# Differential attention heads: each map's scores in one three-bank PSUM tile, with one maximum, one exponential and one combination over 1152 columns

## The chip, the core and the metric

The kernel runs on one core of a Trainium2 chip. A core has a matrix engine (PE, with its weight loads, PEld), a vector engine (DVE), a scalar engine (ACT), GpSimd (POOL), and DMA queues, which are issued from SP here. Each engine works its instructions off in program order and waits on semaphores of the others. Matmul results land in PSUM: 8 banks of 128 partitions x 512 fp32. The metric is the time of one execution in microseconds (us), the median of several runs.

## The reference, cut to what matters

Two layers act on 1152 tokens (128 of a prompt, 1024 of a sample) of width 1024. The first (even) layer is a state-space scan with pooling, the second (odd) layer is attention; the change is in the odd layer's eight differential heads. Each head computes two softmax maps over the same keys and takes one from the other:

```python
def diff_attention(q, k, v, lam):
    scale = DIFF_HD ** -0.5

    def block(qb):
        s = jnp.einsum('bhiqd,bhikd->bhiqk', qb, k).astype(jnp.float32) * scale
        p = jax.nn.softmax(s, axis=-1)
        attn = p[:, :, 0] - lam * p[:, :, 1]
        return jnp.einsum('bhqk,bhkv->bhqv', attn.astype(v.dtype), v)
```

The prompt's 128 queries see 128 keys; the sample's 1024 queries see 1152 keys (1024 of its own and 128 cached ones). Eight pairs of window heads with a sink follow, and an output projection with a residual and a norm.

## The kernel before, in words

Matmuls run in fp16, with every operand split into a high and a low part (three matmuls per product, `mm3`; the score matmuls have both parts of K stacked on the partitions and need two). The PE's order is written out by hand (`manual_schedule`); the orders of DVE, ACT, POOL and SP come from the framework's scheduler, which takes what stands in a `high_priority` block first. Once built, every engine's order is fixed.

`odd` (L1414) lays the work of the odd layer out. `Filler` holds the projections of the next head as generators: 12 chunks per head (k, q, v and the gate z, three chunks of 384 tokens each, each chunk one PSUM bank with 24 matmuls of 384 columns or 72 of 128). `F.take(us)` lays about that much projection work between the attention's matmuls. `diff_head` (L1256) goes through nine blocks of 128 queries: block 0 is the prompt's (128 keys), blocks 1 to 8 have 1152 keys. In a block, for both maps m = 0 and 1:

- Three score chunks of 384 columns (L1280, two matmuls each), each into a bank of its own (`pt("S1")`). Five banks take turns: three of the tag S1, `s4` and `m3`.
- A maximum per chunk on DVE (L1282), a small one over the three (L1286, negated), and an exponential per chunk on ACT (L1289) with its sum, written to SBUF as `p`. A bank is free again once its exponential has read it.
- `F.take(left / 16)`: a sixteenth of the projections that are left. After map 0, also the value products of a block that lies two blocks back (`diff_pv`, 27 matmuls of 128 columns into the bank `sm`, read out by ACT at L1325, squared at L1327).

Then the block is finished: the sums are added (L1298), the factor is built (L1300, L1301), `p[0] + factor * p[1]` is made in three chunks on DVE (L1303), rounded to fp16 on ACT (L1306), the rest taken on POOL (L1307), and both are transposed by a DMA to `PT` (L1227) for the value products.

The projections have two banks (`mm`), one of them being filled while the other is read: by ACT for k and q (L1165, then a shuffle and products on DVE and POOL, L1169 to L1175, and at the end the fp16 copy `qhl`, L1181), by ACT and then DVE for v (L1204, L1205) and z (L1216, L1217). When a head's last value product is in, `diff_pv` builds a reciprocal root on DVE (L1331, then `rsqrt`, L375 to L380, and L1333), and `try_finish` scales nine blocks of the head's output on DVE (L1244 x9); this falls into the first blocks of the next head. New weights are split by ACT (L323) and DVE (L324).

After the eighth head come the window heads (`win_block`), with score banks S1 and value banks `sm` and `s4`; the last two value products of the eighth differential head are laid between the first window blocks' matmuls.

Of the kernel before, what the change touches and what calls it, by code (L numbers as in the profile page):

```python
# [14 lines left out]
ALU = mybir.AluOpType  # L15
# [17 lines left out]
# even layer: the projections between the scans, by group; the fill (us of the tensor engine) of a group and the  # L33
# shares of it before its first step, per stored state, in either half of an output step, and per context state; the
# steps of the storing scan after which M is prepared
# [9 lines left out]
# odd layer: the fill of the first block of a head's queries, behind the first head's projections; the first block of a  # L45
# window head against the others; the score banks
HEAD_FIRST, HEAD_KEEP, HEAD_0 = 1.5, 1.0, 9.0
WIN_FIRST, WIN_SHIFT = 1.5, 1.0
SCORE_BANKS = ("S1", "s4", "S1", "m3", "S1")
NE = 5  # L50
# atanh(z) / z = 1 + s (c0 + c1 s + ...), s = z**2 <= 1/9, to 4e-10
# [20 lines left out]
class Filler:  # L72
    """projections whose matmuls are laid between the attention's and the scans'"""
# [11 lines left out]
    def to_front(self):  # L85
        """the jobs added with front=True from here on come next, behind the one under way"""
        self.pos = 1 if self.begun else 0
# [40 lines left out]
class OutProj:  # L128
    """x_new = x + gate * (g @ w_out), 128 columns of the result at a time; with rby the first half of g is
    scaled by it (per token) on its way out of PSUM"""  # L130
# [21 lines left out]
    def part(self, nb, ps, c0, c1, i):  # L152
        """the i-th k-tile of the order"""
# [6 lines left out]
    def begin(self, n, nb=0):  # L160
        """up to the n-th k-tile of block nb, all chunks of tokens"""
# [24 lines left out]
    def run(self, xres, ssq, chunk_done, chunks, before=None):  # L186
        """the rest; chunk_done(x tiles, first, last token) once a chunk is whole"""
# [34 lines left out]
class Builder:  # L222
# [75 lines left out]
    def pt(self, tag, shape=(P, 512)):  # L298
# [3 lines left out]
        p, b = (self.ps, 2 if tag == "mm" else 1) if tag in ("mm", "m3") else (self.ps2, self.psb[tag])  # L302
        return p.tile(list(shape), F32, tag=tag, bufs=b, name=self.nm("ps" + tag))

    # ---------------------------------------------------------------- weights
    def load_w(self, src, nk=KD, n=P, scale=None, rows=None, pool=None):
        """[128, nk, n] fp32 weights -> (hi, lo) fp16 of 64 * w (* a column scale, or one per k-tile)."""
# [19 lines left out]
    def mm3(self, out, ah, al, bh, bl, start, stop):  # L327
        """out (+)= (ah + al).T @ (bh + bl) without the product of the two low parts"""
# [5 lines left out]
    def g_proj(self, src, hs, evac, pre=None):  # L334
        """channel-major projection: evac(psum [128 ch, 384 tok], first, last token); pre: its weights, and the
# [920 lines left out]
    def diff_head(self, h, F):  # L1256
# [8 lines left out]
        for b in range(NCH):  # L1265
# [30 lines left out]
            with self.tc.high_priority():  # L1296
# [8 lines left out]
                for c0, c1 in part:  # L1305
                    nc.scalar.activation(phl[:, c0:c1], p[0][:, c0:c1], AF.Copy)  # L1306
# [337 lines left out]
```

## Time and profile before

| what | value |
|---|---|
| time, median of 3 runs | 2302.61 us (2298.39 to 2303.87) |
| profiled execution, from the first to the last instruction | 2299.9 us, granted PE clock 0.958 on the mean |
| PE busy over the span | 2025.4 us (88%) |
| DVE busy | 1658.4 us (72%) |
| ACT busy | 1275.3 us (55%) |
| POOL busy | 1070.7 us (47%) |
| first score matmul of the differential heads | at 1023.1 us |
| first score matmul of the window heads | at 1709.3 us |

A row of a group reads: line, engine, operation, output tile <- input tiles, shapes, count | busy us, mean ns of one | idle time of the engine just before, and what ended it. A row of a timeline reads: start, length, engine, line, tiles, and in brackets the idle time before it with what ended that. PE's lengths overlap: matmuls are pipelined, and the pitch from start to start is what one costs. A window's row gives each engine's busy time and count, the granted PE clock, the DMA share and GB/s.

### The profile page before, as it was taken

How to read it: one execution, taken by the hardware profiler on the slowest of the kernel's cores; microseconds unless marked ns; L12 is line 12 of the kernel's file. 1: busy time of each engine (PE TensorE's matmuls, PEld its weight loads, DVE VectorE, ACT ScalarE, POOL GpSimd, SP SyncE). 2: the span in 40 equal slices, each digit the busy share in tenths (PEclk: the TensorE clock that was granted, in tenths of full speed). 3: DMA queues.
4: the chain of work that ended last, by engine and by line, in shares of the span. 5: the costliest groups of instructions: out<-in, count | busy, mean ns of one | idle time of the engine just before them, and what ended most of it. 6: DMA issues, size and time to landing. Idle time of an engine off the chain costs nothing. (4 is left out here: it accounts for less than half of the span.)

```text
span 2299.9 us, 51010 instructions
## 1 busy us (share of the span) xinstructions
PE 2025.4 (88%) x20258; PEld 1449.5 (63%) x20258; DVE 1658.4 (72%) x3483; ACT 1275.3 (55%) x3432; POOL 1070.7 (47%) x997
## 2 busy tenths in 40 slices
PE   5997788788999999989898898998978898988997
PEld 2654475654657555657586686676666777676566
DVE  5878989789585544768978978878888767663334
ACT  5575656666464211447666666676667756673321
POOL 1378677876774100154534435445446656552001
PEclk9998899998999999999999999999999999999999
DMA  7221514224657412136445455455466867889412
GB/s 283 63 82 53 152 46 122 78 82 132 224 180 209 172 63 85 63 100 121 98 109 123 90 121 121 89 122 110 96 121 137 162 145 152 168 170 206 147 47 83
DMA packets 434990, 283.17 MB, mean 123 GB/s; under 512 B 374432, under 2 KB 385216, under 8 KB 434752
## 3 DMA queue, kind: packets, MB, share of 16 engines
q1 hardware_dynamic: 433776, 279.34, 49.0%
q8 instruction: 158, 2.59, 0.5%
q10 hardware_dynamic: 976, 0.58, 0.1%
q14 instruction: 80, 0.66, 0.1%
HBM read 133.38 MB, written 29.05 MB: 71 GB/s over the span
## 5 line engine op out<-in xcount | busy, mean ns | idle before, releaser
L330 PE MATMUL psmm<-h,whl 128*128 128x384 f16 (+1 forms) x1104 | 366.4, 333 | 9.7 <-DVE V L1205 3.8
L331 PE MATMUL psmm<-h,whl 128*128 128x384 f16 (+1 forms) x1104 | 365.7, 332 | 2.4 <-DVE h L507 1.7
L332 PE MATMUL psmm<-h,whl 128*128 128x384 f16 (+1 forms) x1104 | 365.1, 332 | 0.0
L330 PE MATMUL psmm<-whl,h 128*128 128x128 f16 x1920 | 346.2, 225 | 0.0
L331 PE MATMUL psmm<-whl,h 128*128 128x128 f16 x1920 | 345.8, 224 | 0.0
L332 PE MATMUL psmm<-whl,h 128*128 128x128 f16 x1920 | 345.5, 224 | 0.0
L331 PEld LDWEIGHTS <-whl 128*128 128x128 f16 x2256 | 224.8, 100 | 155.4 <-issue 30.7
L332 PEld LDWEIGHTS <-whl 128*128 128x128 f16 x2256 | 224.4, 99 | 155.1 <-issue 16.0
L330 PEld LDWEIGHTS <-whl 128*128 128x128 f16 x2256 | 225.5, 100 | 149.4 <-issue 21.5
L1307 POOL TENSOR_TENSOR phl<-p,phl 128x1152 f16<-128x1152 f32 (+1 forms) x72 | 158.4, 2200 | 242.4 <-ACT phl L1306 208.7
L324 DVE SCALAR_TENSOR_TENSOR whl<-w,whl 128x512 f16<-128x512 f32 x248 | 211.3, 875 | 67.8 <-ACT whl L323 67.4
L330 PEld LDWEIGHTS <-h 128*128 128x128 f16 x2520 | 251.2, 100 | 9.5 <-issue 3.8
L331 PEld LDWEIGHTS <-h 128*128 128x128 f16 x2520 | 251.1, 100 | 7.6 <-issue 1.9
L332 PEld LDWEIGHTS <-h 128*128 128x128 f16 x2520 | 250.9, 100 | 0.0
L1289 ACT ACTIVATE p<-psS,sms 128x384 f32<-128x384 f32 (+1 forms) x240 | 136.4, 570 | 100.3 <-DVE sms L1286 100.2
L1387 POOL TENSOR_TENSOR phl<-p,phl 128x1024 f16<-128x1024 f32 (+2 forms) x72 | 134.2, 1864 | 120.4 <-ACT phl L1386 120.1
L323 ACT ACTIVATE whl<-w 128x512 f16<-128x512 f32 x248 | 140.0, 609 | 81.3 <-PE psmm L332 44.7
L1173 POOL TENSOR_TENSOR sw<-sw,sin 128x384 f32<-128x384 f32 (+1 forms) x78 | 84.7, 1087 | 147.7 <-DVE sw L1172 134.9
L1280 PEld LDWEIGHTS <-Q 128*128 128x128 f16 x800 | 73.7, 98 | 126.0 <-issue 91.3
L504 POOL TENSOR_TENSOR h<-mt,h 128x384 f16<-128x384 f32 (+2 forms) x32 | 29.3, 925 | 251.6 <-ACT h L503 251.6
L1280 PE MATMUL psS<-K,Q 128*128 128x384 f16 (+1 forms) x480 | 109.5, 323 | 41.6 <-ACT p L1289 41.4
L1303 DVE SCALAR_TENSOR_TENSOR p<-p,sms,p 128x384 f32<-128x384 f32 (+1 forms) x200 | 136.7, 718 | 2.0
(394 smaller groups left out, 6242.5 us busy)
## 6 DMA issues: line engine op xcount, KB each, us to landing
w<-in_wod SPq DMA_DIRECT2D x52, 512.0 KB, 3.7
w<-in_wev SPq DMA_DIRECT2D x40, 512.0 KB, 4.1
E<-csrow SPq DMA_DIRECT2D x36, 512.0 KB, 4.0
Q<-qhl SPq DMA_DIRECT2D x64, 288.0 KB, 4.5
go_dr<-gl SPq DMA_DIRECT2D x15, 576.0 KB, 3.2
wada<-in_w_ada SPq DMA_DIRECT2D x32, 256.0 KB, 5.8
o<-in_w_ada SPq DMA_DIRECT2D x16, 512.0 KB, 5.9
xT<-in_w_ada SPq DMA_DIRECT2D x16, 512.0 KB, 5.9
```

Source lines behind the costliest of these rows:

```text
L323: nc.scalar.activation(hl[:, 0, a:e], w[:, a:e], AF.Copy if scale is None else AF.Identity, scale=sc)
L324: nc.vector.scalar_tensor_tensor(hl[:, 1, a:e], w[:, a:e], sc, hl[:, 0, a:e], ALU.mult, ALU.subtract)
L330: mm(out, ah, bh, start=start, stop=False)
L331: mm(out, ah, bl, start=False, stop=False)
L332: mm(out, al, bh, start=False, stop=stop)
L504: nc.gpsimd.tensor_tensor(h[:, 1, a:b], o, h[:, 0, a:b], ALU.subtract)
L1173: nc.gpsimd.tensor_tensor(sw[:, o:], sw[:, o:], self.sinT[:, a:b], ALU.mult)
L1280: nc.tensor.matmul(sv, q[:, m, x, qs], k[:, m, o + c0:o + c1], start=x == 0, stop=x == 1)
L1289: nc.scalar.activation(pm[:, c0:c1], ss[j], AF.Exp, bias=nb, accum_out=sm[:, i:i + 1])
L1303: nc.vector.scalar_tensor_tensor(p[0][:, c0:c1], p[1][:, c0:c1], sm[:, 2:3], p[0][:, c0:c1], ALU.mult, ALU.add)
L1307: nc.gpsimd.tensor_tensor(phl[:, w:2 * w], p[0][:, :w], phl[:, :w], ALU.subtract)
L1387: nc.gpsimd.tensor_tensor(phl[:, 2 * w:4 * w], p, phl[:, :2 * w], ALU.subtract)
```

## The change

The score banks of the differential heads become two tiles of three banks each (tag `S`, 6 banks). A map's scores for all 1152 columns go into one tile (matmuls of 512, 512 and 128 columns). One maximum and one exponential run over the whole row. Map 0's exponential goes to SBUF as before; map 1's is written back over its own scores in PSUM and read from there by one combination of 1152 columns, and one fp16 copy follows. The chunk maxima's reduction and the adding of the chunk sums go. The other two banks (`mm`) serve the projections and, in turn with them, the value products. When the eight heads are done, all value products that still wait are issued, the pool of `S` tiles is closed, and the window heads get banks as before. `m3` is a bank of the even layer's pool, and then of the window heads' pool.

```diff
@@ pt
-        p, b = (self.ps, 2 if tag == "mm" else 1) if tag in ("mm", "m3") else (self.ps2, self.psb[tag])
+        p, b = (self.ps, 2) if tag == "mm" else (self.ps2, self.psb[tag])
@@ prologue
-        self.evps.enter_context(self.psum("evps", ss=4, ada=1))
+        self.evps.enter_context(self.psum("evps", ss=4, ada=1, m3=1))
@@ diff_head
+            o = TC if b else 0
-            sm = self.wt([P, 16], F32, tag="sms", bufs=6)
-            part = ((0, P),) if b == 0 else CH3
+            sm = self.wt([P, 8], F32, tag="sms", bufs=6)
             for m in range(2):
-                ss = []
-                mx = self.wt([P, 4], F32, tag="mx", bufs=4)
+                sv = self.pt("S", [P, 1536])[:, :w]
                 nb = sm[:, m:m + 1]
-                for j, (c0, c1) in enumerate(part):
-                    sv = self.pt("S1")[:, :c1 - c0]
-                    o = TC if b else 0
+                for c0 in range(0, w, 512):
+                    c1 = min(c0 + 512, w)
                     for x in range(2):
-                        nc.tensor.matmul(sv, q[:, m, x, qs], k[:, m, o + c0:o + c1], start=x == 0, stop=x == 1)
-                    with self.tc.high_priority():
-                        nc.vector.tensor_reduce(out=mx[:, j:j + 1], in_=sv, axis=AX.X, op=ALU.max)
-                    ss.append(sv)
-                pm = self.wt([P, T], F32, tag="p", bufs=4)
+                        nc.tensor.matmul(sv[:, c0:c1], q[:, m, x, qs], k[:, m, o + c0:o + c1], start=x == 0, stop=x == 1)
+                e = self.wt([P, T], F32, tag="p", bufs=4)[:, :w] if m == 0 else sv
                 with self.tc.high_priority():
-                    nc.vector.tensor_reduce(out=nb, in_=mx[:, 0:len(part)], axis=AX.X, op=ALU.max, negate=True)
-                    for j, (c0, c1) in enumerate(part):
-                        i = 8 + m * 3 + j
-                        nc.scalar.activation(pm[:, c0:c1], ss[j], AF.Exp, bias=nb, accum_out=sm[:, i:i + 1])
-                p.append(pm)
+                    nc.vector.tensor_reduce(out=nb, in_=sv, axis=AX.X, op=ALU.max, negate=True)
+                    nc.scalar.activation(e, sv, AF.Exp, bias=nb, accum_out=sm[:, 4 + m:5 + m])
+                p.append(e)
...
-                n = len(part)
-                nc.vector.tensor_reduce(out=sm[:, 4:6], in_=sm[:, 8:14].rearrange("p (a b) -> p a b", a=2)[:, :, 0:n],
-                                        axis=AX.X, op=ALU.add)
                 nc.vector.reciprocal(sm[:, 6:8], sm[:, 4:6])
                 nc.vector.scalar_tensor_tensor(sm[:, 2:3], sm[:, 4:5], self.nlam, sm[:, 7:8], ALU.mult, ALU.mult)
-                for c0, c1 in part:
-                    nc.vector.scalar_tensor_tensor(p[0][:, c0:c1], p[1][:, c0:c1], sm[:, 2:3], p[0][:, c0:c1],
-                                                   ALU.mult, ALU.add)
-                for c0, c1 in part:
-                    nc.scalar.activation(phl[:, c0:c1], p[0][:, c0:c1], AF.Copy)
-            nc.gpsimd.tensor_tensor(phl[:, w:2 * w], p[0][:, :w], phl[:, :w], ALU.subtract)
+                nc.vector.scalar_tensor_tensor(p[0], p[1], sm[:, 2:3], p[0], ALU.mult, ALU.add)
+                nc.scalar.activation(phl[:, :w], p[0], AF.Copy)
+            nc.gpsimd.tensor_tensor(phl[:, w:2 * w], p[0], phl[:, :w], ALU.subtract)
@@ odd
-                odps.enter_context(self.psum("odps", S1=3, s4=1, sm=1))
-                self.banks = {"mm": ["m3", "S1", "mm", "mm"]}
+                odps.enter_context(self.psum("dfps", S=2))
+                self.banks = {"mm": ["S", "S", "mm", "mm"]}
...
-                self.banks = {"mm": ["mm"], "S1": list(SCORE_BANKS)}
+                self.banks = {"mm": ["mm"], "sm": ["mm"]}
...
                     self.diff_head(h, F)
+                F.until(("wk", 0))
+                F.until(("q", 8))
+                self.pop(0)
+                odps.close()
+                odps.enter_context(self.psum("odps", S1=3, m3=1, s4=1, sm=1))
                 self.banks = {"mm": ["mm", "mm", "m3"], "sm": ["sm", "s4"]}
```

The rest of the diff drops comments and blank docstrings, so the line numbers of the changed kernel lie a little lower: L1281 is its maximum, L1282 its exponential, L1292 its combination, L1293 its fp16 copy, L1312 the read-out of the value product, L1164 that of a k or q chunk, L1203 that of a v chunk, L1243 the scaling of the head's output. On the PE the change moves nothing: matmul by matmul the same products stand in the same places, with other tiles and other score widths. On ACT and DVE the scheduler lays the rows in another order.

The first place is DVE in the fourth block of the fourth head, where the third head's output is scaled. `psS` are scores, `p` the exponentials of map 0, `raw` and `sw` belong to a q chunk, `og` is the head's output. Before:

```order
L1282 TENSOR_REDUCE mx_16466<-psS_1996_16475 128x1
L1244 SCALAR_TENSOR_TENSOR og_14606<-og_14606,orr_16335,zs_15558 128x128
L1286 TENSOR_REDUCE sms_16421<-mx_16466 128x1
L1244 SCALAR_TENSOR_TENSOR og_14606<-og_14606,orr_16335,zs_15558 128x128 x2
...
L1282 TENSOR_REDUCE mx_16524<-psS_2005_16525 128x1
L1282 TENSOR_REDUCE mx_16524<-pss_2006_16529 128x1
L1282 TENSOR_REDUCE mx_16524<-psS_2007_16533 128x1
L1300 RECIPROCAL sms_16421<-sms_16421 128x2
L1244 SCALAR_TENSOR_TENSOR og_14606<-og_14606,orr_16335,zs_15558 128x128
L1286 TENSOR_REDUCE sms_16523<-mx_16524 128x1
...
L1303 SCALAR_TENSOR_TENSOR p_16435<-p_16479,sms_16421,p_16435 128x384 x3
```

And in the changed kernel, at the same place of the PE's order (its `psS_15862` and `psS_15906` are the score rows that before had 16467 to 16475 and 16525 to 16533):

```order
L1243 SCALAR_TENSOR_TENSOR og_14242<-og_14242,orr_15753,zs_15070 128x128 x5
L1281 TENSOR_REDUCE sms_15825<-psS_15862 128x1
L1243 SCALAR_TENSOR_TENSOR og_14242<-og_14242,orr_15753,zs_15070 128x128
L1171 STREAM_SHUFFLE sw_15879<-raw_15877 128x384
L1173 TENSOR_TENSOR q_1775_15707<-raw_15877,cos_11480 128x384
L1243 SCALAR_TENSOR_TENSOR og_14242<-og_14242,orr_15753,zs_15070 128x128
L1290 RECIPROCAL sms_15825<-sms_15825 128x2
L1243 SCALAR_TENSOR_TENSOR og_14242<-og_14242,orr_15753,zs_15070 128x128
L1291 SCALAR_TENSOR_TENSOR sms_15825<-sms_15825,lms_11493 128x1
L1292 SCALAR_TENSOR_TENSOR p_15833<-psS_15862,sms_15825,p_15833 128x1152
L1281 TENSOR_REDUCE sms_15905<-psS_15906 128x1
```

Before, the next block's maxima stand ahead of this block's combination; now the next block's maximum stands behind the combination, and six of the nine products of L1243 (the first of them one row ahead of these) ahead of this block's second maximum.

The second place is ACT there, up to the read-out of a value product (`og`). `psmm_16497` and `psmm_15884` are the same chunk of q, before and now. Before:

```order
L1289 ACTIVATE p_16479,sms_16421<-psS_1996_16475,sms_16421 128x384
L1289 ACTIVATE p_16537,sms_16523<-psS_2005_16525,sms_16523 128x384
L1289 ACTIVATE p_16537,sms_16523<-pss_2006_16529,sms_16523 128x384
L1165 ACTIVATE raw_16554<-psmm_16497 128x384
L323 ACTIVATE whl_17439<-w_2102_17437 128x512 x2
L1289 ACTIVATE p_16537,sms_16523<-psS_2007_16533,sms_16523 128x384
L1306 ACTIVATE phl_16510<-p_16435 128x384 x3
L1181 ACTIVATE qhl_16561<-q_1965_16289 128x1152
L1325 ACTIVATE og_16015<-pssm_16596,sms_16116 128x128
```

Now:

```order
L1282 ACTIVATE psS_15862,sms_15825<-psS_15862,sms_15825 128x1152
L509 ACTIVATE gl_15778<-og_14242 128x1152
L1293 ACTIVATE phl_15897<-p_15833 128x1152
L1282 ACTIVATE p_15913,sms_15905<-psS_15906,sms_15905 128x1152
L1164 ACTIVATE raw_15928<-psmm_15884 128x384
L322 ACTIVATE whl_16709<-w_1865_16707 128x512 x2
L1180 ACTIVATE qhl_15935<-q_1775_15707 128x1152
L1312 ACTIVATE og_15469<-psmm_15970,sms_15564 128x128
```

The chunk's read-out now stands behind the fp16 copy of the block before it and behind a whole row's exponential. The value product `psmm_15970` (before: `pssm_16596`, in a bank of its own) takes the bank that `psmm_15884` had, since the other of the two is being filled by the next chunk.

The third place is ACT where the last two v chunks of a head are read out (`V`). Before:

```order
L1325 ACTIVATE og_16015<-pssm_16785,sms_16242 128x128
L1327 ACTIVATE osq_16814,oss_16016<-og_16015 128x128
L1289 ACTIVATE p_16829,sms_16709<-psS_2037_16817,sms_16709 128x384
L1204 ACTIVATE V_16569<-psmm_16736 128x384
L1289 ACTIVATE p_16829,sms_16709<-psS_2038_16821,sms_16709 128x384
L1289 ACTIVATE p_16829,sms_16709<-pss_2039_16825,sms_16709 128x384
L1306 ACTIVATE phl_16888<-p_16723 128x384
L1289 ACTIVATE p_16915,sms_16901<-psS_2046_16903,sms_16901 128x384
L1289 ACTIVATE p_16915,sms_16901<-psm_2047_16907,sms_16901 128x384
L1204 ACTIVATE V_16569<-psmm_16860 128x384
```

Now:

```order
L1312 ACTIVATE og_15469<-psmm_16137,sms_15668 128x128
L1314 ACTIVATE osq_16166,oss_15470<-og_15469 128x128
L1282 ACTIVATE psS_16168,sms_16069<-psS_16168,sms_16069 128x1152
L1203 ACTIVATE V_15943<-psmm_16088 128x384
L1293 ACTIVATE phl_16231<-p_16077 128x1152
L1282 ACTIVATE p_16247,sms_16239<-psS_16240,sms_16239 128x1152
L1203 ACTIVATE V_15943<-psmm_16203 128x384
```

Here too a chunk's read-out (`psmm_16203`) stands behind a whole row's exponential; on the PE six matmuls of 128 columns lie between that chunk's end and the value product `psmm_16312`, which takes its bank.

More of the change, by code (lines that the diff above doesn't have):

```diff
@@ L48 @@
 WIN_FIRST, WIN_SHIFT = 1.5, 1.0
-SCORE_BANKS = ("S1", "s4", "S1", "m3", "S1")
 NE = 5
```

## The prediction

> **What bounds the kernel now.** I looked first at the stretch of the differential heads in the table of windows, then at two heads in the middle.
>
> ```profile
> span 2299.9 us, 51010 instructions
> ```
> ```profile
> 1126.50:1215.20 88.70, 78.89 (x896) 62.34 (x896) 74.50 (x178) 58.20 (x177) 40.01 (x25) 0.96 0.51 109
> 1215.20:1303.90 88.70, 78.91 (x896) 62.36 (x896) 74.46 (x178) 58.19 (x177) 40.00 (x25) 0.96 0.50 110
> 1023.00:1709.30 686.30, 605.58 (x6809) 474.35 (x6807) 576.80 (x1362) 453.68 (x1375) 311.11 (x187) 0.96 0.51 109
> ```
>
> The eight heads take 686.3 us, the middle ones 88.7 us each and alike. PE is busy for 78.9 us of a head, DVE for 74.5, ACT for 58.2. PE's waits in this stretch are few and of one kind:
>
> ```profile
> PE psS L1280 <- ACT p L1289: 41.4, 19, 4.3
> PE psm L1280 <- ACT p L1289: 32.6, 9, 5.6
> PE pss L1280 <- ACT p L1289: 3.6, 9, 1.2
> ```
>
> 77.6 us in all, always a score matmul whose bank an exponential has not yet read. PE's timeline shows where in a head:
>
> ```profile
> 1215.19 0.48 PE L1280 MATMUL psS<-K,Q 128*128 128x384 f16 x2 [2.66 <-ACT p L1289]
> ...
> 1221.80 0.48 PE L1280 MATMUL psS<-K,Q 128*128 128x384 f16 x2 [2.56 <-ACT p L1289]
> ...
> 1235.72 0.80 PE L1280 MATMUL psm<-K,Q 128*128 128x384 f16 x2 [4.34 <-ACT p L1289]
> 1236.32 0.31 PE L330 MATMUL psmm<-whl,h 128*128 128x128 f16 x1
> 1236.42 0.31 PE L331 MATMUL psmm<-whl,h 128*128 128x128 f16 x1
> ```
> ```profile
> 1234.20:1241.10 6.90, 5.38 (x48) 5.04 (x47) 4.97 (x11) 3.87 (x12) 5.29 (x3) 0.51 0.76 148
> ```
>
> Three waits of 9.55 us at a head's start and none later. Behind the longest the clock is at 0.51 for 6.9 us, and matmuls of 128 columns come every 0.107 us; in full clock it is:
>
> ```profile
> 1681.50 0.22 PE L330 MATMUL psmm<-whl,h 128*128 128x128 f16 x1
> 1681.55 0.22 PE L331 MATMUL psmm<-whl,h 128*128 128x128 f16 x1
> ...
> 1669.73 0.33 PE L330 MATMUL psmm<-h,whl 128*128 128x384 f16 x1
> 1669.89 0.33 PE L331 MATMUL psmm<-h,whl 128*128 128x384 f16 x1
> ```
>
> 0.055 us (0.163 for 384 columns). From the wait's end to the end of the slow stretch (some 5.4 us) half is lost, 2.7 us. So a head is 76.5 us of PE work plus 12.2 us. The burst is DVE's: the last head's output is scaled there while k and q are turned and weights split. Its rows, with the others I need (mean ns of one; then minimum/median/maximum):
>
> ```profile
> L1282 DVE TENSOR_REDUCE mx<-psS 128x1 f32<-128x384 f32 x232 | 123.1, 547 | 14.4 <-PE psS L1280 13.8
> L1289 ACT ACTIVATE p<-psS,sms 128x384 f32<-128x384 f32 x232 | 133.6, 577 | 98.7 <-DVE sms L1286 98.7
> L1289 ACT ACTIVATION_READ_ACCUMULATOR p<-psS,sms 128x1 f32 x239 | 48.2, 202 | 0.0
> L1303 DVE SCALAR_TENSOR_TENSOR p<-p,sms,p 128x384 f32<-128x384 f32 x192 | 131.2, 719 | 1.9
> L1306 ACT ACTIVATE phl<-p 128x384 f16<-128x384 f32 x192 | 92.8, 524 | 73.5 <-DVE p L1303 73.4
> L510 ACT ACTIVATE gl<-og 128x1152 f16<-128x1152 f32 x8 | 9.3, 1165 | 0.0
> L1307 POOL TENSOR_TENSOR phl<-p,phl 128x1152 f16<-128x1152 f32 x64 | 155.0, 2421 | 241.8 <-ACT phl L1306 208.2 <-issue 33.6
> L1165 ACT ACTIVATE raw<-psmm 128x384 f32<-128x384 f32 x49 | 23.7, 484 | 3.6 <-PE psmm L332 3.6
> L1204 ACT ACTIVATE V<-psmm 128x384 f16<-128x384 f32 x24 | 11.7, 489 | 0.0
> L1205 DVE SCALAR_TENSOR_TENSOR V<-psmm,V 128x384 f16<-128x384 f32 x24 | 13.2, 552 | 19.3 <-ACT V L1204 19.3
> L1244 DVE SCALAR_TENSOR_TENSOR og<-og,orr,zs 128x128 f32<-128x128 f32 x72 | 55.8, 806 | 0.1
> L1174 DVE TENSOR_TENSOR q<-raw,cos 128x384 f32<-128x384 f32 x34 | 26.2, 769 | 0.0
> ```
> ```profile
> L1282 DVE TENSOR_REDUCE mx<-psS x240: 278/547/558, 1023.4 to 1709.3; 128x1 f32<-128x384 f32 x112, 128x1 f32<-128x128 f32 x8
> L1289 ACT ACTIVATE p<-psS,sms x240: 357/578/597, 1023.9 to 1711.5; 128x384 f32<-128x384 f32 x119, 128x128 f32<-128x128 f32 x1
> L1303 DVE SCALAR_TENSOR_TENSOR p<-p,sms,p x200: 332/610/2727, 1034.0 to 1714.6; 128x384 f32<-128x384 f32 x96, 128x128 f32<-128x128 f32 x4
> L1217 DVE SCALAR_TENSOR_TENSOR zs<-zs,psmm x21: 539/548/555, 1080.0 to 1627.8; 128x384 f32<-128x384 f32 x21
> L1244 DVE SCALAR_TENSOR_TENSOR og<-og,orr,zs x63: 323/339/2446, 1130.5 to 1677.0; 128x128 f32<-128x128 f32 x63
> L375 DVE TENSOR_SCALAR rqy<-oss x7: 159/2535/2543, 1119.6 to 1651.4; 128x9 int32<-128x9 int32 x7
> ```
>
> **The change part by part.** *Sizes.* From 128 to 384 columns a maximum grows by 269 ns, 1.05 ns a column: 1152 take 1.35 us. The exponential grows by 0.86 ns a column: 1.24 us, plus 0.2 for its sum. The fp16 copy is like L510's, 1.17. Scores cost PE the same: 4 x 0.217 + 2 x 0.055 against 6 x 0.163, 0.98 us.
>
> The combination has one operand in PSUM, as L1217, whose longest run is 555 ns; L1303, all in SBUF, runs from 332 to 2727. I take 1.35 us; it lies between that and 3 x 0.719 = 2.16. The Trainium skill, page "SBUF — State Buffer", section "Who interferes with whom", says that a DVE instruction with at most one SBUF input, outside the two-port modes, does not contend with GpSimd; the steady L1217 agrees. By the rule it is 1.35 whatever POOL does; by L1303's mean it would be 2.16, and each chain below 0.8 us longer.
>
> No row shows an exponential written to PSUM. Bounds: 1.15 us (ACT reads PSUM and writes SBUF in 0.484 for a copy, 0.09 under the exponential) and twice 1.24; I take 1.24, the nearest row.
>
> *What is saved.* A full block loses on DVE 6 x 0.547 + 2 x 0.149 (the small maximum) + 3 x 0.719 and gains 3 x 1.35, some 1.7 us less; ACT loses 6 x 0.779 + 3 x 0.524 and gains 2 x 1.44 + 1.17, 2.2 less. Over 64 blocks that is 109 and 141 us, but PE waits for neither outside the burst: there alone it could count.
>
> *What takes the waits' place.* A score tile is free after the exponential (map 0) or the combination (map 1), and is wanted two maps later, over 8 us after its scores: mostly no wait. But the value products now share two banks with the projections. One that comes while a chunk is being filled needs the bank of the chunk before, so it waits for that chunk's read-out; that stands on ACT behind a whole row's exponential, which needs a maximum that stands on DVE behind a combination. PE is in order: behind the value product wait the next scores and chunks.
>
> The v stretch (third place in the order), from the end of `psS_16168`: PE has 24 matmuls, a value product, scores, 45 and 6 matmuls: 1.33 + 1.50 + 0.98 + 2.50 + 0.33 = 6.6 us until `psmm_16312`. The chain: maximum until 1.5, exponential until 2.9, factor and a v remainder until 3.8, combination until 5.1, the next maximum 6.4, its exponential 7.7, read-out on ACT 8.1 and on DVE 8.65. PE waits 2.0 us. The v chunk before it, worked the same way, waits 1.3; a z chunk 0.4. In the k stretch the value product ahead of the burst arrives after 6.9 us and its chain (with a shuffle and a product in the exponential's shade) ends at 8.0 to 8.6: 1.5. The second map of block 0 wants the tile of block 8's combination, which stands behind a z remainder and two weight splits: chain 5.5 to 6.1 against 3.9: 2.0. Short waits: 7.2 us a head, all new.
>
> The burst (first and second place), from the end of block 2's second scores (`psS_15782`): that maximum stands behind a weight split and ends at 2.35. The root (L375 meets POOL) pushes the combination to 6.2 until 7.6. PE wants the tile at 7.0: 0.65. Then block 3's first maximum until 8.95, a q chunk that meets POOL's 2.42 us until 12.9, six products until 15.2, the second maximum 16.5, three products, shuffle, product and factor 19.0, combination 20.4, block 4's maximum 21.7, exponential 22.9, read-out of `psmm_15884` 23.4. PE is held for 0.85 at a chunk that wants the read-out of block 0's value product, and reaches `psmm_15970` at 16.45: 6.95. The burst: 8.45 us, where before it was 9.55; the half clock's 2.7 stays.
>
> Whether a wait lowers the clock is read from the quoted rows: behind the waits of 2.66 and 2.56 us two score matmuls take 0.48 us, behind that of 4.34 they take 0.80. The 6.95 will lower it, the short ones should not.
>
> *The end of the heads.* The last value products now stand ahead of the first window scores:
>
> ```profile
> 1711.11 0.27 PE L1363 MATMUL psS<-K,Q 128*128 128x128 f16 x2 [1.54 <-ACT p L1289]
> ```
> ```profile
> PT<-phl SPq DMA_TRANSPOSE x144, 4.6
> ```
>
> From the last scores: maximum, exponential, factor, combination, copy, remainder and transposition are 1.35 + 1.44 + 0.4 + 1.35 + 1.17 + 2.42 + 4.6, 13 us with the hops. Two value products (3 us) lie beside it: 10 us idle, some 2 of half clock, less an estimated 4 that the window's first blocks no longer wait (1.54 above and its like): +8.
>
> **The sum.** Per head +7.2 - 1.1 = +6.1; for the six alike starts 37. The last head has no z and less fill: +4. Head 0 has no burst and loses its small bank waits against new ones: -1. With the end's +8: +48 on 2299.9, 2348. The profiled execution lies 2.7 us under the median of 2302.6; so 2351.
>
> **The rivals.** *Much the same, 2296 to 2309*: the burst is half as long as I walk it (-4 a head) and the short waits lose a third. For it: DVE has 1.7 us less per block.
>
> *Faster, 2277*: DVE's burst fits under the PE. Its place is the chain to `psmm_15970`, its price 12.2 us a head; it decides where that chain is 7 us shorter. If POOL met none of them, the nine products would take 0.34 instead of 0.81 on the mean and L375 0.16 instead of 2.54: 6.6 us, just about. Then a head changes by 7.2 - 12.2 = -5, seven by -35, with +8 and -1: 2302.6 - 28 = 2275 or so. Against it: the same POOL rows stand there.
>
> *Slower still, about 2420*: short waits too lower the clock. The Trainium skill's clock page, section "A second HAM failure mode: psum-queue depth-cycling", describes just such oscillation from cycling banks. Six short waits a head, each followed by 3.4 us at half rate, cost 1.7 each, 10 a head, 70 in all. Against it: the 2.66 us wait left the clock at 1.
>
> *Slower by the exponential in PSUM, about 2385*: at 2.48 us the chains of four waits and the burst lengthen by 1.24: some 5 a head, 35.
>
> **How the numbers follow.** Forecast 0.66, much the same 0.08, faster 0.14, low clock 0.05, slow exponential 0.07. Below 2275 I leave half of the faster case, above 2400 the low clock: the range is 2275 to 2400; the forecast's own is 2325 to 2385. A measurement tells about 0.3% from no change (7 us): slower 0.78, same 0.08, faster 0.14.
>
> **What would show it.** In the profile of the changed kernel PE should wait at L1309 (value product) for ACT or DVE read-outs of `psmm`, some 7 us once per head with half clock behind it, and 1 to 2 us at v and k; waits of L1278 should fall below 20 us; DVE's busy time should fall by about 110 us, ACT's by 140. I am wrong if the wait at L1309 in the burst is under 2 us, or if no value product waits behind an exponential.

## The result, and the profile after

The changed kernel takes **2341.13 us** (median of 4 runs, 2339.42 to 2342.15) against 2303.18 us before (4 runs, 2298.39 to 2303.87): a ratio of **1.016**, 95% interval 1.0147 to 1.0172, so 1.6% slower. Two further kernels below turned out to have the same instruction order as the changed one, and one the same order on all compute engines as before. They measured 2334.53 and 2335.59, and 2300.52: the cost of the change lies between 1.4% and 1.6%, and one program's time shifts by up to 7 us from one series to another.

The page of the changed kernel, its span and its busy time by engine:

```profile
span 2338.6 us, 49724 instructions
PE 2038.3 (87%) x20258; PEld 1446.4 (62%) x20258; DVE 1592.3 (68%) x2883; ACT 1210.8 (52%) x2792; POOL 1065.9 (46%) x997
```

DVE and ACT are busy for 66.1 and 64.5 us less than before, and the kernel is 38.7 us longer. Where the waits are now is in the view of PE's waits from 1020 to 1760 us (tile and line that waited <- what it waited for: total us, times, longest):

```profile
PE psmm L1309 <- ACT raw L1164: 54.7, 14, 7.0
PE psmm L1309 <- DVE V L1204: 19.5, 8, 7.3
PE psS L1278 <- DVE p L1292: 10.8, 8, 2.6
PE psmm L329 <- ACT og L1312: 8.8, 7, 4.4
PE psmm L1309 <- DMA PT<-phl: 7.3, 2, 5.0
```

Before, every long wait of a middle head stood at a score matmul (L1280) for an exponential. Now the value product (L1309) waits for the read-out of *another* tile, a k or q chunk (`raw`), a v chunk (`V`) or, for 2.5 us in all, a z chunk: it takes the bank that such a chunk had. The reverse stands in the fourth row, where a projection waits for a value product's read-out (`og`).

PE's timeline, the waits over 0.3 us of one middle head and the longest of the next:

```profile
1220.13 0.22 PE L1309 MATMUL psmm<-V,PT 128*128 128x128 f16 x1 [1.17 <-ACT raw L1164]
1231.02 1.15 PE L1278 MATMUL psS<-K,Q 128*128 128x512 f16 x6 [1.25 <-DVE p L1292]
1233.88 0.32 PE L329 MATMUL psmm<-h,whl 128*128 128x384 f16 x1 [0.74 <-ACT og L1312]
1246.91 0.27 PE L1309 MATMUL psmm<-V,PT 128*128 128x128 f16 x1 [6.99 <-ACT raw L1164]
...
1269.93 0.22 PE L1309 MATMUL psmm<-V,PT 128*128 128x128 f16 x1 [2.00 <-DVE V L1204]
...
1338.39 0.27 PE L1309 MATMUL psmm<-V,PT 128*128 128x128 f16 x1 [7.00 <-ACT raw L1164]
```

From one long wait to the next a head takes 91.5 us (88.7 before), and it waits 1.17 + 1.25 + 0.74 + 6.99 + 2.00 = 12.15 us (9.55 before). The table of windows gives the clock there (stretch and its length, then busy time of PE, PEld, DVE, ACT, POOL, and the granted clock):

```profile
1246.90:1338.40 91.50, 79.11 (x896) 60.72 (x896) 65.40 (x101) 49.97 (x97) 39.29 (x25) 0.95 0.53 105
1242.00:1252.20 10.20, 5.29 (x39) 4.19 (x39) 7.89 (x10) 6.30 (x9) 7.42 (x6) 0.50 0.44 115
1260.00:1272.00 12.00, 10.00 (x150) 8.67 (x148) 6.66 (x9) 6.71 (x13) 2.73 (x2) 1.00 0.64 101
```

The clock halves some 2 us into the long wait and stays so until 5.3 us of matmuls have run; across this wait of 2.00 us it stays at 1.

Where the 38.7 us come from is read at the same read-out of a k or q chunk in both traces (there are 78 in each): one just ahead of the first scores, the first that belongs to head 1's filling, the first of the last head's, and one among the first window blocks, after which the lag stays within some 3 us of that. Before:

```profile
1021.85 0.49 ACT L1165 ACTIVATE raw<-psmm 128x384 f32<-128x384 f32 x1 [4.79 <-issue]
1101.15 0.47 ACT L1165 ACTIVATE raw<-psmm 128x384 f32<-128x384 f32 x1
1633.89 0.48 ACT L1165 ACTIVATE raw<-psmm 128x384 f32<-128x384 f32 x1
1765.80 0.50 ACT L1165 ACTIVATE raw<-psmm 128x384 f32<-128x384 f32 x1
```

And after:

```profile
1026.09 0.49 ACT L1164 ACTIVATE raw<-psmm 128x384 f32<-128x384 f32 x1 [4.91 <-issue]
1115.74 0.48 ACT L1164 ACTIVATE raw<-psmm 128x384 f32<-128x384 f32 x1
1663.49 0.48 ACT L1164 ACTIVATE raw<-psmm 128x384 f32<-128x384 f32 x1
1803.59 0.49 ACT L1164 ACTIVATE raw<-psmm 128x384 f32<-128x384 f32 x1
```

The lag is 4.2, 14.6, 29.6 and 37.8 us. So 4.2 us lie ahead of the heads, where both do the same work; head 0 adds **10.4**, six heads **15.0** (2.5 each), the last head and the end of the heads **8.2**.

### The profile page after: what moved, and what is told of

It reads as the page before. It is cut to its first block, busy times and chain, and to the rows that moved or that the text cites. A ratio compares the mean times of both kernels' runs of the same rounds, so it can differ in the third digit from the quotient of the medians.

```text
span 2338.6 us, 49724 instructions
## 1 busy us (share of the span) xinstructions
PE 2038.3 (87%) x20258; PEld 1446.4 (62%) x20258; DVE 1592.3 (68%) x2883; ACT 1210.8 (52%) x2792; POOL 1065.9 (46%) x997
## 5 line engine op out<-in xcount | busy, mean ns | idle before, releaser
L329 PE MATMUL psmm<-whl,h 128*128 128x128 f16 x1920 | 334.1, 220 | 4.4 <-ACT og L1312 4.4
L330 PE MATMUL psmm<-whl,h 128*128 128x128 f16 x1920 | 333.8, 220 | 0.0
L331 PE MATMUL psmm<-whl,h 128*128 128x128 f16 x1920 | 333.5, 220 | 0.0
L330 PEld LDWEIGHTS <-h 128*128 128x128 f16 x2520 | 247.1, 99 | 6.1 <-issue 4.5
L329 PEld LDWEIGHTS <-h 128*128 128x128 f16 x2520 | 247.3, 99 | 4.2 <-issue 2.6
L331 PEld LDWEIGHTS <-h 128*128 128x128 f16 x2520 | 247.1, 99 | 0.0
L1281 DVE TENSOR_REDUCE sms<-psS 128x1 f32<-128x1152 f32 (+1 forms) x144 | 176.7, 1231 | 91.7 <-PE psS L1278 91.6
L1309 PE MATMUL psmm<-V,PT 128*128 128x128 f16 x520 | 101.5, 233 | 84.2 <-ACT raw L1164 54.7
L1278 PE MATMUL psS<-K,Q 128*128 128x512 f16 (+1 forms) x800 | 158.8, 335 | 17.3 <-DVE p L1292 10.8
L1293 ACT ACTIVATE phl<-p 128x1152 f16<-128x1152 f32 (+1 forms) x72 | 76.9, 1068 | 116.3 <-DVE p L1292 59.9
```

The lines of the kernel that those rows point to most:

```text
L329: mm(out, ah, bh, start=start, stop=False)
L330: mm(out, ah, bl, start=False, stop=False)
L331: mm(out, al, bh, start=False, stop=stop)
L1278: nc.tensor.matmul(sv[:, c0:c1], q[:, m, x, qs], k[:, m, o + c0:o + c1], start=x == 0, stop=x == 1)
L1281: nc.vector.tensor_reduce(out=nb, in_=sv, axis=AX.X, op=ALU.max, negate=True)
L1293: nc.scalar.activation(phl[:, :w], p[0], AF.Copy)
```

## The experiments

Theory: the loss is that value products and projections share two banks, so that PE waits for read-outs that stand behind whole rows on ACT and behind DVE's burst. Rival: the coarse grain itself, two score tiles in place of five banks and a next maximum behind a whole combination. Every time is a median with the kernel before run beside it.

**Sharing alone.** The kernel before, and its value products in the projections' banks:

```diff
-                self.banks = {"mm": ["mm"], "S1": list(SCORE_BANKS)}
+                self.banks = {"mm": ["mm"], "sm": ["mm"], "S1": list(SCORE_BANKS)}
```

> The kernel before, with one change: value products of the differential heads take the two projection banks; five score banks and pieces of 384 columns stay. If sharing is the loss, PE waits at the value products in the burst and in the v stretch, though less than in the changed kernel since a read-out stands behind pieces of 0.6 us and not rows of 1.2: +8 to +30 us, 2310 to 2333. If grain is the loss, no change: 2298 to 2309.

Measured: 2328.75 us, ratio 1.0108 (1.0088 to 1.0127): **+26 us**. PE's waits in its heads (1020 to 1700 us) are those of the changed kernel:

```profile
PE psmm L1322 <- ACT raw L1165: 24.3, 8, 5.5
PE psmm L1322 <- DVE V L1205: 22.9, 12, 2.2
```

The wait of 2.65 us at the second scores of a head stands at 1225.71 and again at 1318.00: a pitch of 92.3 us, more than the 91.5 of the changed kernel. Sharing alone is enough for the longer middle heads; the rest of the change gives a little back there (0.8 us a head). It is not the whole loss, though the sums are close. At the four read-outs used above, the lag of this kernel is 4.6, 6.9, 30.0 and 29.0 us: head 0 adds 2.3, six heads 23.1, and the end takes 1.0 back. So most of the 10.4 us of head 0 and all of the 8.2 of the end need the rest of the change.

**The coarse grain alone, in part.** The kernel before with one combination and one fp16 copy of 1152 columns, all in SBUF:

```diff
-                for c0, c1 in part:
-                    nc.vector.scalar_tensor_tensor(p[0][:, c0:c1], p[1][:, c0:c1], sm[:, 2:3], p[0][:, c0:c1],
-                                                   ALU.mult, ALU.add)
-                for c0, c1 in part:
-                    nc.scalar.activation(phl[:, c0:c1], p[0][:, c0:c1], AF.Copy)
+                nc.vector.scalar_tensor_tensor(p[0][:, :w], p[1][:, :w], sm[:, 2:3], p[0][:, :w], ALU.mult, ALU.add)
+                nc.scalar.activation(phl[:, :w], p[0][:, :w], AF.Copy)
```

> The kernel before, with one combination and one fp16 copy of 1152 columns instead of three of 384 each, all in SBUF; scores, maxima, exponentials and banks as before. If PE does not wait for the vector engine outside the burst, the time stays within 7 us of 2303. If long instructions as such hold up the read-outs and maxima behind them, PE's waits at scores grow: 2310 to 2325. In either case the combination's mean is over 2.0 us if it meets POOL as the pieces did (3 x 0.719), against 1.415 with its operand in PSUM.

Measured: 2311.40 us, ratio 1.0031 (1.0019 to 1.0044): +7 to +9 us, near the edge of what can be told, and at the low end of the second expectation. Its wait of 2.79 us at a head's start comes again after 89.6 us (88.7 before), and PE's waits at the scores of the heads are 85.8 us in all (77.6 before). So this part of the coarse grain has a small price of its own. The price of the combination was expected wrongly: a mean of 1.425 us all in SBUF, not over 2.0, with a longest of 2.143. One combination is drawn out by POOL more seldom than three pieces were (together 2.16 in the mean): only 1 of the 64 began while POOL was at work, against 25 of the 192 pieces.

**Value products out of the projections' banks, three ways.** First into 128 unused columns of the block's own first score tile; then the same, but behind the second map's scores:

```diff
-                sv = self.pt("S", [P, 1536])[:, :w]
+                st = self.pt("S", [P, 1536])
+                sv = st[:, :w]
...
+                    self.room = st[:, 1408:1536]
                     self.pop(2)
+                    self.room = None
...
-        po = self.pt("sm")
+        po = self.pt("sm") if self.room is None else self.room
```

> The changed kernel, but the value products of a differential head go into 128 unused columns of the block's first score tile (three banks of 512 columns hold 1152 scores), so the two projection banks serve projections alone. If the loss comes from value products and projections sharing two banks, PE's waits at the value products for read-outs of other tiles (77 us in the profile of the changed kernel: 54.7 behind raw, 19.5 behind V, 2.5 behind zs) go; the vector engine's burst at a head's start stays, so some 2 to 5 us of the 7.0 come back as waits at scores: pitch of a head 85 to 89 us against 91.5, time 2295 to 2320. If it is the coarse grain (two score tiles in place of five banks, a next maximum behind a whole combination), what leaves the value products comes back at the scores: 2335 to 2345.

> The changed kernel, with the value product moved behind the scores of the block's second map and written into 128 unused columns of the first map's score tile, whose exponential is done by then. So nothing waits for a fresh exponential, and the projection banks serve projections alone. If sharing of banks is the loss, PE's waits at the value products for raw, V and zs go, some of the burst comes back at scores or chunks (3 to 5 us a head): pitch 84 to 89 us, time 2280 to 2315. If the coarse grain of two score tiles is the loss, they come back in full at the scores: 2335 to 2345.

Measured: 2382.88 us, ratio 1.0346 (1.0331 to 1.0362), and 2347.16 us, ratio 1.0186 (1.0165 to 1.0206). The waits for read-outs of projections are gone from both, but a new one took their place. From the first of them:

```profile
PE psS L1313 <- ACT p L1284: 105.4, 61, 4.4
```

The value product now waits in nearly every block for the exponential that reads the same bank (61 times from 1020 to 1700 us, up to 4.4 us). Placed later it still does in 34 places (48.7 us), and scores wait for its read-out in 21 (27.7 us). The third way gave it a bank of its own and put both maps into one tile of five banks, the second map's exponential into SBUF:

```diff
-                sv = self.pt("S", [P, 1536])[:, :w]
+                sv = self.row5[:, 1408 * m:1408 * m + w]
...
-                e = self.wt([P, T], F32, tag="p", bufs=4)[:, :w] if m == 0 else sv
+                e = self.wt([P, T], F32, tag="p", bufs=4)[:, :w]
```

> The changed kernel's whole rows without the shared banks: the two maps of a block in one tile of five banks (columns 0 to 1151 and 1408 to 2559), one maximum, one exponential and one combination of 1152 columns, the second map's exponential into SBUF, value products in a bank of their own, projections alone in theirs, and no drain at the end of the heads. If sharing of banks is the loss, PE's waits at value products for raw, V and zs go and what stays are the waits at scores of the kernel before: 2290 to 2315. If the coarse grain is the loss, the waits come back at the scores: 2325 to 2345.

Measured: 2384.14 us, ratio 1.0364 (1.0340 to 1.0388). No value product waits for a projection any more, but scores wait for the exponential of the map just before them, which lies in the same tile:

```profile
PE psR L1278 <- ACT p L1282: 113.5, 48, 3.8
```

All three missed their purpose: each brings a wait of its own as large as the one it removes, so none says what whole rows would cost with banks enough. Two tiles of three banks, two for projections and one for value products are nine, and there are eight: that form was not tried. What they do show is that a tile with a next user within one map of its exponential (a map is some 5 us of a head) can cost more than the sharing.

**The burst.** Is the 7 us wait DVE's chain? A first attempt at both kernels handed out the nine products that scale the last head's output one by one, in the text of the program:

> The changed kernel, with the nine products that scale the last head's output (0.572 us each in the mean) no longer in one row on the vector engine, but one behind every map from the third block on. If the 7.0 us wait of the burst is that engine's chain, it falls by about 5 us and the half clock behind it mostly goes: 5 to 7 us a head, seven heads: 2290 to 2306. If the chain is set by something else (the scalar engine waiting for GpSimd, the turning of k and q), the wait stays over 5 us: 2328 to 2341.

> The kernel before, with the same spreading of the nine products. If the three waits of 9.55 us at a head's start are the vector engine's burst, 3 to 7 us a head go, the half clock behind them included: 2255 to 2282. If they are set elsewhere: 2295 to 2305.

Measured: 2335.59 us, ratio 1.0140 (1.0115 to 1.0165), and 2300.52 us, ratio 0.9982 (0.9968 to 0.9997), with the wait unchanged at 6.98 us in the changed kernel. They say nothing of the theory: the scheduler issues what is ready, and put the products back where they had been. The second attempt queues each behind a maximum, an order that it must keep:

```diff
+                if b > 3 and self.late:
+                    with self.tc.issue_after(mi):
+                        self.late.popleft()()
                 F.take(HEAD_FIRST if b == 0 else left / 16)
```

> The changed kernel, with each of the nine products queued on the vector engine behind the maximum of a map from the fifth block on (an order that the scheduler must keep), so that none stands in the burst; the order on PE is the same. If the 7.0 us wait is the vector engine's chain, it loses the products that ran in it (2.0 us for six in a row, then 0.3, 1.1 and 1.1): 7.0 becomes 2.5, and of the half clock behind it 1 to 3 us go: 5 to 7 us a head, 2298 to 2316 against 2335 to 2341 for runs of the changed kernel's own order. If the chain is set by the scalar engine or GpSimd: the wait over 5 us, time 2328 to 2341.

> The kernel before, with the same order for the nine products; nothing else moves. If its waits at a head's start (9.55 us, and 2.7 us of half clock) are the vector engine's burst, the 4.3 us wait goes, and the half clock behind it: 4 to 7 us a head, 2256 to 2276. If the turning of k and q and the weight splits alone hold it: 2290 to 2305.

Measured: the changed kernel 2312.89 us, ratio 1.0048 (1.0031 to 1.0065), **22 to 28 us less** than the three measurements of its own order; the kernel before **2286.96 us, ratio 0.9936 (0.9922 to 0.9951)**, the fastest version found. In the changed kernel the wait became

```profile
1235.87 0.27 PE L1326 MATMUL psmm<-V,PT 128*128 128x128 f16 x1 [3.35 <-ACT raw L1166]
```

3.35 us instead of 6.99, against 2.5 expected, and the pitch 88.1 instead of 91.5. To see why, DVE's timeline in the changed kernel ahead of its wait (scores for the second maximum were in at 1232.2):

```profile
1232.61 2.27 DVE L1173 TENSOR_TENSOR q<-raw,cos 128x256 f32<-128x256 f32 x1
1234.81 0.69 DVE L379 SCALAR_TENSOR_TENSOR orr<-rqa,rqy 128x9 f32<-128x9 f32 x1
1235.53 0.17 DVE L1320 TENSOR_SCALAR orr<-orr 128x9 f32<-128x9 f32 x1
1235.74 2.01 DVE L1243 SCALAR_TENSOR_TENSOR og<-og,orr,zs 128x128 f32<-128x128 f32 x6
1237.67 1.34 DVE L1281 TENSOR_REDUCE sms<-psS 128x1 f32<-128x1152 f32 x1
...
1242.45 1.42 DVE L1292 SCALAR_TENSOR_TENSOR p<-psS,sms,p 128x1152 f32<-128x1152 f32 x1
1243.79 1.35 DVE L1281 TENSOR_REDUCE sms<-psS 128x1 f32<-128x1152 f32 x1
```

The six products hold the maximum up for 2 us, and three behind it (0.33, 1.08 and 1.07 us) hold the combination; after the last row come an exponential (1.22 us) and the chunk's read-out (0.48), and PE goes on at 1246.91. With the products elsewhere the turning of q (2.27 us) and the root's last steps stay in the chain. With them moved, by the four read-outs, the changed kernel's head 0 still adds 10.7 us and the end of its heads 9.2, while the six heads between are together 7.7 us shorter than those of the kernel before.

In the kernel before, the wait of 4.34 us fell to 2.35 to 2.58, and most of the half clock went with it (granted clock of a head 0.98 to 1.00 against 0.96). Its pitch is 85.0 to 85.5 us; the time fell by 14 us and not by the 27 to 47 expected. In the middle head the wait of 2.66 us stayed, that of 2.56 went, and one of 2.05 us came behind the burst. Both kernels with their products moved, like with like, are 25.9 us apart: the change costs 1.1% there too.

Then the steps that make the products' factors were queued later too, in the kernel before:

```diff
+        def root():
+            r = self.wt([P, 16], F32, tag="orr", bufs=2)
...
+        if self.spread:
+            self.late.append(root)
+        else:
+            root()
```

> The kernel before, with the nine products as in the last experiment and also the twelve small steps that make their factors (2.0 us for the first where it meets GpSimd, about 0.17 each for the others) queued behind the fifth block's first maximum; PE's order is that of before. If these steps hold the waits of 2.65 and 1.0 us at a head's start, these go: 3 us a head, 2262 to 2276 against 2287 with the products alone. If they only move the delay to the fifth block, where the weight splits are: 2280 to 2292.

Measured: 2304.44 us, ratio 1.0008 (0.9998 to 1.0017), above both expectations: all that the products had gained is lost. DVE's timeline at the new place, and POOL's:

```profile
1229.18 2.33 DVE L378 TENSOR_SCALAR rqy<-rqy 128x9 int32<-128x9 int32 x1
1231.54 2.28 DVE L380 TENSOR_TENSOR rqa<-rqy,oss 128x9 f32<-128x9 f32 x1
...
1233.94 0.55 DVE L1296 TENSOR_REDUCE mx<-psm 128x1 f32<-128x384 f32 x1
1234.41 1.01 DVE L1296 TENSOR_REDUCE mx<-psS 128x1 f32<-128x384 f32 x2
```
```profile
1228.67 2.81 POOL L1324 TENSOR_TENSOR phl<-p,phl 128x1152 f16<-128x1152 f32 x1
1231.44 2.36 POOL L1184 TENSOR_TENSOR qhl<-q,qhl 128x1152 f16<-128x1152 f32 x1
```

Two steps on nine columns, 0.17 us each where nothing meets them, last until POOL's long instruction beside them ends; the maxima stand behind, and PE waits 6.37 us there in every head, with half clock. What a burst costs is here not its count of instructions but what meets POOL in it.

**The end of the heads.** Two kernels put a projection ahead of the last value products. The first named one (the window's v) that the last head's filling had already finished, so the program's order did not change:

> The changed kernel, with the first window value projection (three chunks, some 12 us of PE) computed ahead of the last value products instead of between the first window blocks. If the end of the heads costs 7 to 8 us because PE waits there for the last block's chain (waits of 4.96 and 2.35 us and half clock behind them), these waits go and the time falls by 4 to 9 us: 2332 to 2337. If the projection is missed among the window blocks, the waits there grow by as much: 2338 to 2344.

Measured: 2334.53 us, ratio 1.0143 (1.0125 to 1.0161), a repeat of the changed kernel. The second took the last head's gate projection:

```diff
                 F.until(("q", 8))
+                add_z(7)
+                F.until(("z", 7))
                 self.pop(0)
```

> The changed kernel, with the last differential head's gate projection (12 us of PE, which otherwise comes between the first window blocks) computed ahead of the last value products. If the end of the heads costs 7 to 8 us because PE waits there for the last block's chain (4.96 and 2.35 us at the value products), these waits go and the time falls by 4 to 9 us: 2328 to 2335. If the projection is missed among the window blocks, their waits for exponentials grow by as much: 2336 to 2344.

Measured: 2346.25 us, ratio 1.0188 (1.0166 to 1.0209). The waits of 4.96 and 2.35 us for the transposition are gone, and the work is missed among the window blocks, more than expected:

```profile
1808.54 0.37 PE L1350 MATMUL psS<-K,Q 128*128 128x128 f16 x2 [15.00 <-DMA Q<-qhl]
```

The next window head's q now comes with no other work behind which its turning and its transposition could lie: 15 us of waiting for 7.3 removed.

## Why the prediction was right, and where it was not

The forecast was 2351 us, with its own range 2325 to 2385; measured were 2341. The mechanism was the one forecast: value products that wait for the read-outs of projections, a long wait of 6.95 us (6.99) at the start of every middle head with half clock behind it, and the banks' sharing priced by itself at +26 us. The sum was nearer than its terms: **+48 forecast on the span, +38.7 found**. Two terms were off in opposite directions, 22 us too much and 11 too little, so that it came so near is in part luck.

- *Sizes.* Right, by the groups of the changed kernel (line, shapes, count | busy, mean ns | idle before):

```profile
L1281 DVE TENSOR_REDUCE sms<-psS 128x1 f32<-128x1152 f32 x128 | 172.8, 1350 | 87.3 <-PE psS L1278 87.2
L1292 DVE SCALAR_TENSOR_TENSOR p<-psS,sms,p 128x1152 f32<-128x1152 f32 x64 | 90.5, 1415 | 2.8
L1282 ACT ACTIVATE p<-psS,sms 128x1152 f32<-128x1152 f32 x64 | 78.0, 1219 | 14.2 <-DVE sms L1281 10.8
L1282 ACT ACTIVATE psS<-psS,sms 128x1152 f32<-128x1152 f32 x64 | 76.2, 1191 | 71.7 <-DVE sms L1281 71.4
L1293 ACT ACTIVATE phl<-p 128x1152 f16<-128x1152 f32 x64 | 74.4, 1163 | 98.8 <-DVE p L1292 59.9 <-issue 35.4 <-POOL sw L1172 3.4
```

  1.35, 1.42, 1.22 and 1.16 us against 1.35, 1.35, 1.24 and 1.17. The unknown one, an exponential written back to PSUM, takes 1.19 us: no price, and the rival built on 2.48 us falls. The combination with an operand in PSUM never lasted over 1.419 us, though POOL was already at work when 6 of the 64 began, and for 0.95 us more; the pieces in SBUF went up to 2.727. The rule of the Trainium skill, page "SBUF — State Buffer", section "Who interferes with whom", that a DVE instruction with at most one SBUF input, outside the two-port modes, does not contend with GpSimd, holds here.
- *Busy time.* DVE and ACT were to lose 110 and 140 us and lost 66 and 65. The busy times of the groups that the change touches, each group taken by itself, add up as forecast (DVE 379.3 to 269.9 us, ACT 402.6 to 264.5); but instructions of different groups overlap at their ends (above, a maximum of 0.55 us ends 0.08 us after the next has started), and an engine's busy time counts the overlap once. The rest of DVE's work hardly changed (busy 1333.9 us before, 1336.0 after). Sums over groups overstate here what joining instructions saves.
- *The burst*, 8.45 us forecast, 1.25 + 0.74 + 6.99 = 8.98 found, each part at its place (the step of the root that meets POOL is L1318, 2.00 us, and not the one that met it before). That it is DVE's chain is shown by the reordered products, which took 3.64 of the 6.99 us with them.
- *Short waits, 7.2 us a head*: found 2.00 at the v end (2.0), 1.17 at the k stretch (1.5), 0.24 at the z chunk (0.4), and none at the first v chunk (1.3) and at block 0's second map (2.0). **This is the step that failed.** Block 0's second map was to wait for the tile of block 8's combination. Its scores start while that combination still reads:

```profile
1203.49 1.42 DVE L1292 SCALAR_TENSOR_TENSOR p<-psS,sms,p 128x1152 f32<-128x1152 f32 x1
1203.53 0.28 PE L1278 MATMUL psS<-K,Q 128*128 128x128 f16 x2
```

  So they are in the other tile, which block 0's own first exponential had left at 1203.14; how the tiles came to be given out so is not shown. The earlier v chunk was worked "the same way" as the last one, whose read-out stands on ACT behind a copy and an exponential. The first chunk's read-out stands ahead of them:

```profile
1256.37 0.48 ACT L1203 ACTIVATE V<-psmm 128x384 f16<-128x384 f32 x1
1256.74 1.17 ACT L1293 ACTIVATE phl<-p 128x1152 f16<-128x1152 f32 x1
```

  DVE's part of it ends at 1258.24, and the next value product comes at 1258.62 and does not wait. A head is then +2.6 us of waits instead of +6.1, 2.5 by the lag: 15 us for six heads, not 37.
- *Head 0, -1 us*: +10.4. This term was not walked at all, and is read from the trace alone. PE waits 7.26 us there for a v chunk, until 1069.70. ACT, POOL and DVE ahead of that:

```profile
1062.85 1.16 ACT L1180 ACTIVATE qhl<-q 128x1152 f16<-128x1152 f32 x1 [4.41 <-POOL q L1174]
...
1064.21 1.17 ACT L1282 ACTIVATE psS<-psS,sms 128x1152 f32<-128x1152 f32 x1
...
1065.56 0.48 ACT L1203 ACTIVATE V<-psmm 128x384 f16<-128x384 f32 x1
```
```profile
1058.73 2.68 POOL L1294 TENSOR_TENSOR phl<-p,phl 128x1152 f16<-128x1152 f32 x1
```
```profile
1059.11 2.85 DVE L323 SCALAR_TENSOR_TENSOR whl<-w,whl 128x512 f16<-128x512 f32 x1
...
1069.10 0.55 DVE L1204 SCALAR_TENSOR_TENSOR V<-psmm,V 128x384 f16<-128x384 f32 x1
```

  A weight split beside POOL's remainder lasts 2.85 us and puts the block's second maximum off, to end at 1063.23. ACT, in order, stands for 4.41 us at the fp16 copy of a turned head, which waits for POOL behind the same remainder; the map's exponential is queued behind it and starts 1 us after its maximum is there. The chunk's read-out on ACT follows at once, and its part on DVE stands behind a combination and the next maximum until 1069.10. The forecast had this last piece, but no chain of it has ACT standing for POOL.
- *Last head and end, +4 and +8*: 8.2 together. The waits for the last transposition are there (4.96 and 2.35 us).
- *Ahead of the heads*: 4.2 us that no term held. Two other profiles of the same order begin the heads' scores at 1023.4 and 1025.0 us where this one begins them at 1027.3, so this is spread between executions.
- *Low clock at short waits*, the rival near 2420: no. The waits of 2.00 us left the clock at 1 in all heads but one (0.50 from 1453.7 to 1457.0 us); one of 1.95 us in the last head was followed by 3.4 us of half clock too. *Faster* (2277 at its head, 2275 by its own sum) and *much the same*: the burst did not fit under the PE; with its products out of the way the changed kernel still is 0.5% slower.

## What to carry to other kernels

Before joining instructions to save an engine's time, ask whether PE waits for that engine anywhere, and what the banks that the joined form needs were doing: here 66 us of DVE time bought nothing, and one bank fewer by itself cost 26. In a full PSUM the worth of a bank is the time between its last write and its read-out, and a read-out is as late as the longest thing queued ahead of it, on any engine in its chain. Where a burst makes the wait, pin work that nobody waits for behind what somebody does, and look first at what it will meet on POOL: the same nine products, put later, made both kernels faster, and a dozen shorter steps put at a worse place lost it all.

## What was not expected of the hardware

- A DVE step on 9 columns lasts 0.17 us alone and 2.28 to 2.33 us beside a POOL instruction of 2.4 to 2.8 us, ending when that one ends: it waits its whole length out. The first of them has one SBUF input. The Trainium skill, page "SBUF — State Buffer", section "Who interferes with whom", names both causes: two SBUF inputs, and a `tensor_scalar` in a two-port mode, with the shared ports held for a whole instruction; the rows agree, though in which mode that first step ran is not shown.
- A wait of one length halved the clock in one head and not in the next. Two heads of the kernel before with its products moved, behind waits of 2.66 and 2.65 us:

```profile
1213.90:1217.10 3.20, 2.73 (x9) 1.32 (x9) 3.20 (x8) 2.71 (x9) 1.87 (x2) 0.50 0.38 110
1299.90:1303.10 3.20, 3.20 (x21) 1.90 (x21) 3.20 (x6) 2.70 (x8) 1.54 (x3) 1.00 0.16 38
```

  So length alone does not decide it near 2.6 us. The Trainium skill, page "TensorE: Matmul & The Clock Gate", section "What's actually happening", describes activity windows of 3413 ns that run on whatever the program does; the half-clock stretches here, 3.4 to 10.2 us long, agree with one to three of them.
